# A two-layer hybrid diffusion trunk on one core: transposes held back behind products, and a new order of the last MLP groups and of the tiles that begin the next layer

## The chip, the core and the metric

The kernel runs on one core of a Trainium2 chip. The metric is device microseconds (us) of one execution, as the median of several. Five engines work side by side, each through its own instructions in order: PE (TensorE: matrix products and transposes), DVE (VectorE), ACT (ScalarE), POOL (GpSimd) and SP (SyncE, which issues transfers). An instruction whose operands are not ready holds up everything behind it on its engine.

## The reference, cut to what matters

The program is a trunk of two layers over 1024 latent tokens and a prefix of 256 context tokens, model width 1024, all in fp32.

```
for l in range(DEPTH):                       # DEPTH = 2
    h_lat = rms_norm(x, g_attn_pre[l]) * (1.0 + sc1) + sh1      # h_ctx alike, from ctx
    y_lat, y_ctx = hybrid_mixer(h_lat, h_ctx, not last, w_in[l], ...)
    x = x + gt1 * rms_norm(y_lat, g_attn_post[l])
    h = rms_norm(x, g_mlp_pre[l]) * (1.0 + sc2) + sh2
    x = x + gt2 * rms_norm(sq_relu_mlp(h, w_mlp1[l], w_mlp2[l]), g_mlp_post[l])
    if not last: ctx = ...                   # the same two steps for the context
```

`hybrid_mixer` projects its input once (`w_in`). Four gated DeltaNet heads take q, k, v (after a short convolution and silu; q and k normalized per token) and a gate z; each head solves small triangular systems per chunk of 64 tokens and scans over the chunks. Two more branches take their own columns of the projection: a gated linear recurrence (LRU, gated by a gelu) and a latent attention (MLA, from kv and cq columns). `w_out` joins the branches. The MLP is `square(relu(h @ w1)) @ w2` with 4096 hidden units. Context reads only context, and the last layer makes no context output. The result is the latent stream.

## The kernel before, in words

**Blocks and products.** Tokens lie along the columns, in three blocks: `"c"` (256 context tokens), 0 and 1 (512 latent tokens each); `BL` is c, 0, 1. Every weight tile of 128x1024 is fetched by SP (512 KB), copied by ACT into a high part and subtracted by POOL into a low part (`weight`, L138 on POOL). A product (`mm3`, L230) is 24 matmuls where the contraction is 1024: eight slices, each as high x high, high x low and low x high. In the second MLP projection it is 12 matmuls. A product writes one PSUM bank. The tiles of the input projection rotate over three banks, `mm` (two buffers) and `d` (`pd`).

**Who orders the instructions.** The Python code gives the program order, and a list scheduler with a cost estimate then places each engine's instructions by priority, in program order unless `later(n)` sets a stretch of code back by n. A running engine just follows that list. `put_behind(n, insts)` (L196) ties PE instructions of a side computation to the n-th `mm3` that the program issues after them: they stand right behind that product's last matmul.

**A mixer's input tiles.** `qk_tile` (k with transposed copy, q without) and `v_tile` run a product per block, then per block the convolution on ACT and DVE, `silu2` (DVE `T`, L147), and two or four 128x128 transposes on PE into the one bank `st` (L443 for k and q, L462 for v), which ACT reads. `z_tile`, `gelu_tile` and `kv_tile` have one or two evacuations per block: gelu reads its bank twice on ACT. Per head h, `tiles(h)` issues k, q, v and z, and `head(h)` the head. The heads run one after the other. Each begins with small transposes (L624), has a stretch in which DVE is full (an inversion: DVE `X` L690, then PE `pb` L696), and ends with L821. PE fills in with the tiles of the next head while a head waits.

**The order inside layer 1's mixer.** Before the first head come the two gelu tiles, each for blocks 0 and 1, then z of head 0 for both, then tile 0 (coefficients of all heads and the rope part, `evac` in `mixer`) for blocks 0, 1, c, then k, q and v of head 0. Layer 0 begins with tile 0.

**The norms.** `around(b, ...)` closes a sub-layer for a block: `post` (sums of squares by one-column matmuls, L186; a reciprocal root in eleven small DVE operations; its broadcast back by transposes, L192; then eight times an add and a square) and `prenorm` (the same again, then the next input `A`). `behind` gives the four counts for `put_behind`. After w_out the passes are block 0, then blocks 1 and c together.

**The MLP.** Eight groups g of hidden units, each `up` (four weights) and `down` (four weights). Groups 0 and 1 go by pass, 2 to 5 take all blocks together, and the last two, 6 and 7, go block by block so that each block's norm can run under the next block's products: in layer 0 block 0, then 1, then c, the norm of c falling under the first products of layer 1; in layer 1 block 0, then 1. With c alone, every second weight is split by DVE and not by POOL (`weng`).

Of the kernel before, what the change touches and what calls it, by code (L numbers as in the profile page):

```python
# [43 lines left out]
class Trunk:  # L44
# [386 lines left out]
    def qk_tile(self, L, hs, i, ct, blocks, name, tok=False):  # L431

        d = self.dram(name)
        dt = self.dram(name + "t") if tok else None
        ss = self.sp.tile([P, NCH], F32, name=self.nm("ss"))

        def done(b, acc):
            c0, w = GRP[b]
            th = self.silu2(acc)
            self.keep(d, b, acc)  # L440
            ps = self.G()
            for j in range(w):
                self.nc.tensor.transpose(ps[:, j * P:(j + 1) * P], acc[:, j * P:(j + 1) * P], self.ident)  # L443
            for j in range(w):
                self.act(th[:, j * P:(j + 1) * P], ps[:, j * P:(j + 1) * P], AF.Square, accum_out=ss[:, c0 + j:c0 + j + 1])
            self.ts(ss[:, c0:c0 + w], ss[:, c0:c0 + w], 4 * EPS, ALU.add)
            if tok:
                self.act(th, ps[:, :w * P])
                self.keep(dt, b, th)
        self.conv_tile(L, hs, i, SM["gconv"][0] + 4 * ct, blocks, done)  # L450
        return d, ss, dt

    def v_tile(self, L, hs, i, ct, blocks, name):
# [3 lines left out]
        def done(b, acc):  # L457
            w = GRP[b][1]
            self.silu2(acc)
            ps = self.G()  # L460
            for j in range(w):
                self.nc.tensor.transpose(ps[:, j * P:(j + 1) * P], acc[:, j * P:(j + 1) * P], self.ident)  # L462
            t = self.T()[:, :w * P]
# [34 lines left out]

    def kv_tile(self, L, hs, i, name):

        d = self.dram(name)

        def evac(b, ps):
# [5 lines left out]
            self.keep(d, b, t)  # L509
        self.w_in_tile(L, hs, i, BL, evac)  # L510
        return d

# [522 lines left out]
    def mixer(self, L, hs, obl):  # L1035
# [22 lines left out]
        lg = [self.dram(f"lg{t}") for t in range(2)]  # L1058

        if l:  # L1060
            for t in range(2):
                self.gelu_tile(L, hs, 6 + t, obl, lg[t])
            self.z_tile(L, hs, 8, obl, zd[0])
        self.w_in_tile(L, hs, 0, [0, 1, "c"] if l else BL, evac)
        self.gdn_coeffs(L, ba)
# [5 lines left out]
        def tiles(h):  # L1071
# [3 lines left out]
                       self.v_tile(L, hs, i0 + 2, 3 * h + 2, BL, f"v{h}")))  # L1075
            if h or not l:
                self.z_tile(L, hs, 8 + h, obl, zd[h])

# [5 lines left out]
        def xtile(t):  # L1084
            xg.append((self.lx_tile(L, hs, 4 + t, t, f"lx{t}"), lg[t]))
            if not l:
                self.gelu_tile(L, hs, 6 + t, obl, lg[t])

        def kvq():
            pk["kvn"] = self.kv_tile(L, hs, 1, "kvn")  # L1090
            pk["cqn"] = self.cq_tiles(L, hs, 2, obl, "cqn")
# [6 lines left out]
        head(3)  # L1098
        kvq()
        self.close(self.ap)  # L1100
        side = self.side
# [44 lines left out]
    def layer(self, L, hs, xsrc, xdst_mid, xdst_end, nextL):  # L1146
# [10 lines left out]

        def weng(bl, i):

            return nc.vector if bl == ["c"] and i % 2 else None  # L1160

        def around(b, acc, ss, which, x, dst, Ln, nwhich, behind):


            with self.actor("s", (self.tp, 4), ["a", "b" if which and b == "c" else "d"]):
                s2 = self.post(b, acc, ss, L, which, x, dst, Ln is not None, behind[:2])
# [6 lines left out]
        for bl in passes:  # L1173
# [9 lines left out]
            for b in bl:  # L1183
                h2[b] = around(b, acc[b], ss[b], 0, xs[b], xdst_mid, L, 1,
                               {0: (1, 2, 6, 7) if last else (1, 3, 8, 10), 1: (1, 2, 6, 7), "c": (2, 3, 8, 9)}[b])

# [4 lines left out]
        def up(bl, g):  # L1191
            hid = [{} for _ in range(4)]
            for f in range(4):
                w = self.weight(self.I["w_mlp1"][l, 4 * g + f], weng(bl, f))
                for b in bl:
                    n = BLK[b][1]
                    ps = self.M4(n)
                    self.mm3(ps, w, h2[b], range(KD))

                    big = n == 512 or bl == ["c"]  # L1200
                    a = lp.tile([P, 2, 512] if big else [P, 2, n], F32R, tag="hid" if big else "hidc",
                                bufs=8 if big else 4, name=self.nm("hid"))[:, :, :n]
                    r = self.T(0)[:, :n]
# [7 lines left out]
        def down(bl, g, hid):  # L1211
            for mp_ in range(4):
                w = self.weight(self.I["w_mlp2"][l, g, mp_], weng(bl, mp_))
                for mi in range(2):
# [20 lines left out]
        for g in range(2, NG - 2):  # L1235
            down(obl, g, up(obl, g))
        for bl in [[b] for b in obl[-2:] + obl[:-2]]:
            b = bl[0]
            hid = [up(bl, g) for g in (NG - 2, NG - 1)]
            if b == 0:  # L1240
                xs = {}
            for b2 in ([0, 1] if b == 0 else [b] if b == "c" else []):
                xs[b2] = self.fetch(xdst_mid, b2, self.ap, "Ac" if b2 == "c" else "A", 8 if b2 == "c" else 16)
            ss[b] = self.S(BLK[b][1])
            for g in (NG - 2, NG - 1):
                down(bl, g, hid[g - NG])
            hn[b] = around(b, acc[b], ss[b], 1, xs[b], xdst_end, nextL, 0,
                           {0: (2, 3, 7, 8), 1: (0, 0, 0, 0) if last else (2, 4, 9, 11), "c": (1, 2, 3, 4)}[b])
        self.close(lp)
# [184 lines left out]
```

## Time and profile before

| | |
|---|---|
| median of 3 runs | 3834.73 us (3834.34 to 3836.51) |
| the profiled execution's own time | 3835.08 us |
| its span in the profile | 3833.3 us, so 1.8 us lie around it |
| mean granted clock of TensorE | 0.958 |
| busy: PE, DVE, ACT, POOL | 91%, 55%, 43%, 34% of the span |

The stages of the profiled execution, by the start of their first PE instruction: layer 0's first head 154 us, the last head's end 687 us, w_out from 1003 us, layer 1's first product 2097.4 us, its first head 2205 us, the last head's end 2736 us, w_out from about 2982 us.

How to read the rows: "PE pst L443 <- DVE T L147: 22.1, 12, 2.6" in the table of waits says that PE instructions of line 443 that write `pst` stood idle for 22.1 us in all, 12 times, at most 2.6 us, until DVE had written `T` in line 147. A row of the timeline gives the start, the duration, the instruction with output and inputs, the number run together, and in brackets the idle time ahead of it with what ended it. `pst`, `pa`, `pb`, `pd`, `plr`, `mm` are PSUM banks. In a table by windows, "PEclk" is the clock that TensorE was granted as a share of the full one.

### The profile page before, as it was taken

How to read it: one execution, taken by the hardware profiler on the slowest of the kernel's cores; microseconds unless marked ns; L12 is line 12 of the kernel's file. 1: busy time of each engine (PE TensorE's matmuls, PEld its weight loads, DVE VectorE, ACT ScalarE, POOL GpSimd, SP SyncE). 2: the span in 40 equal slices, each digit the busy share in tenths (PEclk: the TensorE clock that was granted, in tenths of full speed). 3: DMA queues.
4: the chain of work that ended last, by engine and by line, in shares of the span. 5: the costliest groups of instructions: out<-in, count | busy, mean ns of one | idle time of the engine just before them, and what ended most of it. 6: DMA issues, size and time to landing. Idle time of an engine off the chain costs nothing. (4 is left out here: it accounts for less than half of the span.)

```text
span 3833.3 us, 51463 instructions
## 1 busy us (share of the span) xinstructions
PE 3505.4 (91%) x19236; PEld 2741.0 (72%) x19236; DVE 2106.1 (55%) x4351; ACT 1648.3 (43%) x3477; POOL 1314.7 (34%) x919
## 2 busy tenths in 40 slices
PE   5999898798998999999997989996798999999998
PEld 3777687344687888888877777774455778888886
DVE  6667757666265155555266587677576371421124
ACT  3555464455454322212354455544555453222242
POOL 4211311335475211111466321113334674222253
PEclk9999999898999999999998999997798999999998
DMA  5221222232432222232334222212002433311143
GB/s 182 94 83 66 83 97 76 91 100 64 151 105 88 67 83 94 88 94 89 128 109 138 99 81 82 77 65 87 31 24 74 153 107 94 96 47 46 52 139 99
DMA packets 164922, 347.13 MB, mean 91 GB/s; under 512 B 15552, under 2 KB 74304, under 8 KB 164672
## 3 DMA queue, kind: packets, MB, share of 16 engines
q1 hardware_dynamic: 164672, 343.85, 27.6%
q8 instruction: 151, 2.47, 0.3%
q14 instruction: 99, 0.81, 0.1%
HBM read 277.99 MB, written 65.80 MB: 90 GB/s over the span
## 5 line engine op out<-in xcount | busy, mean ns | idle before, releaser
L138 POOL TENSOR_TENSOR wl<-wr,wh 128x1024 fp32r<-128x1024 f32 x280 | 679.9, 2429 | 1664.2 <-ACT wh L135 931.0
L230 PE MATMUL mm<-A,wh 128*128 128x512 f32 (+1 forms) x3008 | 709.9, 379 | 12.3 <-DVE A L138 6.3
L135 ACT ACTIVATE wh<-wr 128x1024 fp32r<-128x1024 f32 x288 | 304.8, 1058 | 833.0 <-PE mm L230 328.1
L230 PEld LDWEIGHTS mm<-A,wh 128*128 128x128 f32 x3008 | 522.9, 194 | 108.0 <-ACT A L135 8.1
L138 DVE TENSOR_TENSOR hid<-T,hid 128x512 fp32r<-128x512 f32 (+1 forms) x160 | 173.1, 1084 | 448.4 <-ACT hid L135 448.4
L230 PE MATMUL mm<-A,wl 128*128 128x512 f32 (+1 forms) x1504 | 360.8, 373 | 1.5 <-DVE wl L138 1.4
L230 PE MATMUL mm<-hid,wh 128*128 128x512 f32 (+1 forms) x1280 | 302.9, 378 | 8.8 <-ACT T L135 6.8
L230 PEld LDWEIGHTS mm<-A,wl 128*128 128x128 f32 x1504 | 259.8, 191 | 48.0 <-DVE wl L138 1.6
L230 PEld LDWEIGHTS mm<-hid,wh 128*128 128x128 f32 x1280 | 227.8, 191 | 57.1 <-ACT T L135 7.3
L147 DVE SCALAR_TENSOR_TENSOR T<-raw,sm,T 128x512 f32<-128x512 f32 (+4 forms) x240 | 182.1, 760 | 45.4 <-ACT raw L135 24.2
L138 DVE TENSOR_TENSOR acc<-acc,mm 128x512 f32<-128x512 f32 (+1 forms) x140 | 88.5, 632 | 214.9 <-PE mm L230 214.2
L230 PE MATMUL pd<-A,wh 128*128 128x512 f32 (+1 forms) x704 | 193.9, 403 | 0.0
L230 PE MATMUL plr<-A,wh 128*128 128x512 f32 (+1 forms) x800 | 185.2, 382 | 0.0
L135 ACT ACTIVATE T<-T 128x512 f32<-128x512 f32 (+1 forms) x243 | 141.6, 583 | 95.2 <-DVE T L147 69.2
L1029 PE MATMUL pd<-Pt,V 128*128 128x512 f32 (+1 forms) x336 | 170.0, 628 | 10.6 <-ACT Pt L135 9.0
L138 POOL TENSOR_TENSOR S<-S,T 128x512 f32<-128x512 f32 (+1 forms) x126 | 163.4, 1299 | 36.7 <-ACT T L135 33.0
L230 PE MATMUL mm<-hid,wl 128*128 128x512 f32 (+1 forms) x640 | 167.2, 379 | 8.1 <-DVE wl L138 8.1
L230 PE MATMUL pb<-A,wh 128*128 128x512 f32 (+1 forms) x800 | 173.0, 367 | 1.2 <-ACT wh L135 1.2
L147 DVE SCALAR_TENSOR_TENSOR ada<-wa,sil,ada 128x256 f32<-128x256 f32 x392 | 168.4, 493 | 7.1 <-DMA wa<-in_w_ada_dram 7.1
L230 PEld LDWEIGHTS plr<-A,wh 128*128 128x128 f32 x800 | 143.6, 188 | 31.2
L230 PE MATMUL plr<-hid,wh 128*128 128x512 f32 (+1 forms) x640 | 153.4, 381 | 13.0 <-DVE hid L138 9.9
L147 DVE SCALAR_TENSOR_TENSOR lr<-lr,lr 128x256 f32<-128x256 f32 x218 | 107.0, 501 | 96.7 <-POOL lr L138 87.6
(365 smaller groups left out, 6843.5 us busy)
## 6 DMA issues: line engine op xcount, KB each, us to landing
wr<-in_w_mlp_dram SPq DMA_DIRECT2D x208, 512.0 KB, 3.5
wa<-in_w_ada_dram SPq DMA_DIRECT2D x96, 512.0 KB, 3.7
wr<-in_w_in_dram SPq DMA_DIRECT2D x48, 512.0 KB, 3.6
wr<-in_w_out_dram SPq DMA_DIRECT2D x32, 512.0 KB, 3.7
A<-y SPq DMA_DIRECT2D x32, 256.0 KB, 3.2
xm<-acc SPq DMA_DIRECT2D x32, 256.0 KB, 3.5
x<-xm SPq DMA_DIRECT2D x16, 512.0 KB, 6.2
kT<-k SPq DMA_DIRECT2D x8, 640.0 KB, 4.2
```

The source lines that it names most:

```text
L135: return self.nc.scalar.activation(out, in_, f, **kw)
L138: return (eng or self.nc.vector).tensor_tensor(out, a, b, op=op)
L147: return self.nc.vector.scalar_tensor_tensor(out, a, s, b, op0=op0, op1=op1)
L230: mm = nc.tensor.matmul(ps, w[wi][:, wk, :], a[:, ai, :], start=n == 0, stop=n == last)
L1029: nc.tensor.matmul(po, V[:, c, :], p, start=ci == 0, stop=ci == len(chunks) - 1)
```

## The change

It has four parts.

- **Transposes.** In `qk_tile` and `v_tile` the transposes go through `put_behind(1 + blocks.index(b), ...)`: those of c stand behind the first product that follows the tile's own, those of block 0 behind the second, of block 1 behind the third (q in layer 1, which has no c, counts 0 and 1). What is still held back at the mixer's end of projections is dropped from the list (`self.held = []`).
- **Last MLP groups of layer 0.** Groups 6 and 7 take c and block 0 together on shared weights (up 6, down 6, up 7, down 7), then block 1 alone (up 6, up 7, down 6, down 7). That is sixteen weight tiles fewer; `weng` goes. The norms are issued for block 0, then c, then, after block 1's products, for block 1. Layer 1 keeps block 0, then 1.
- **First tiles of layer 1.** Block 0 alone of gelu 0, gelu 1 and z of all four heads, then kv of c and 0, then tile 0 for c, 0, 1. The block 1 parts of z, gelu and kv come at the places where these tiles stood before or, for z of head 0, after v of head 0. That is seven weight tiles more.
- **Norms after w_out.** `around` of block 1 stands in `later(60)` and that of c in `later(300)`, with new counts; a pair of PSUM banks changes.

```diff
@@ qk_tile (v_tile alike)
             ps = self.G()
-            for j in range(w):
-                self.nc.tensor.transpose(ps[:, j * P:(j + 1) * P], acc[:, j * P:(j + 1) * P], self.ident)
+            self.put_behind(1 + blocks.index(b), [self.nc.tensor.transpose(
+                ps[:, j * P:(j + 1) * P], acc[:, j * P:(j + 1) * P], self.ident) for j in range(w)])
@@ mixer
+        two = [1] if l else obl
+        pk["kvn"] = self.dram("kvn")
         if l:
             for t in range(2):
-                self.gelu_tile(L, hs, 6 + t, obl, lg[t])
-            self.z_tile(L, hs, 8, obl, zd[0])
-        self.w_in_tile(L, hs, 0, [0, 1, "c"] if l else BL, evac)
+                self.gelu_tile(L, hs, 6 + t, [0], lg[t])
+            for h in range(NH):
+                self.z_tile(L, hs, 8 + h, [0], zd[h])
+            self.kv_tile(L, hs, 1, ["c", 0], pk["kvn"])
+        self.w_in_tile(L, hs, 0, BL, evac)
...
-            if h or not l:
-                self.z_tile(L, hs, 8 + h, obl, zd[h])
+            self.z_tile(L, hs, 8 + h, two, zd[h])
...
-            if not l:
-                self.gelu_tile(L, hs, 6 + t, obl, lg[t])
+            self.gelu_tile(L, hs, 6 + t, two, lg[t])
...
-            pk["kvn"] = self.kv_tile(L, hs, 1, "kvn")
+            self.kv_tile(L, hs, 1, [1] if l else BL, pk["kvn"])
...
         kvq()
+        self.held = []
@@ layer
-            with self.actor("s", (self.tp, 4), ["a", "b" if which and b == "c" else "d"]):
+            with self.actor("s", (self.tp, 4), ["a", "b" if which and b == 1 else "d"]):
...
-                h2[b] = around(b, acc[b], ss[b], 0, xs[b], xdst_mid, L, 1,
-                               {0: (1, 2, 6, 7) if last else (1, 3, 8, 10), 1: (1, 2, 6, 7), "c": (2, 3, 8, 9)}[b])
+                with self.later({0: 0, 1: 60, "c": 300}[b]):
+                    h2[b] = around(b, acc[b], ss[b], 0, xs[b], xdst_mid, L, 1,
+                                   {0: (1, 2, 6, 7) if last else (1, 3, 8, 10), 1: (1, 2, 6, 8), "c": (3, 5, 14, 16)}[b])
...
-        for bl in [[b] for b in obl[-2:] + obl[:-2]]:
-            b = bl[0]
-            hid = [up(bl, g) for g in (NG - 2, NG - 1)]
...
+        for bl in ([[0], [1]] if last else [["c", 0], [1]]):
+            gs = (NG - 2, NG - 1)
+            hid = {g: up(bl, g) for g in gs} if len(bl) == 1 else {}
...
+            for g in gs:
+                down(bl, g, hid.get(g) or up(bl, g))
...
-            hn[b] = around(b, acc[b], ss[b], 1, xs[b], xdst_end, nextL, 0,
-                           {0: (2, 3, 7, 8), 1: (0, 0, 0, 0) if last else (2, 4, 9, 11), "c": (1, 2, 3, 4)}[b])
+            for b in bl[::-1]:
+                hn[b] = around(b, acc[b], ss[b], 1, xs[b], xdst_end, nextL, 0,
+                               {0: (2, 3, 7, 8) if last else (1, 2, 6, 7), 1: (0, 0, 0, 0) if last else (1, 2, 6, 7),
+                                "c": (2, 3, 9, 11)}[b])
```

The order of the instructions shows three places. The first is PE in layer 0's mixer, at the k tile of head 0, before. `pst_781` are the two transposes of its context block; `pd_746` is the tile's own last product (block 1), `mm_840` the first product of the next tile, q.

```order
L230 MATMUL pd_746<-A_490,wl_691 128x512
L230 MATMUL pd_746<-A_494,wl_691 128x512
L443 MATMUL pst_781<-cst,T_772 128x128 x2
L230 MATMUL mm_840<-A_402,wh_836 128x256
L230 MATMUL mm_840<-A_406,wh_836 128x256
```

The same transposes now, as `pst_782`; `mm_841` is the q tile's first product and `mm_867` its second.

```order
L230 MATMUL mm_841<-A_426,wl_838 128x256
L230 MATMUL mm_841<-A_430,wl_838 128x256
L443 MATMUL pst_782<-cst,T_773 128x128 x2
L230 MATMUL mm_867<-A_434,wh_837 128x512
L230 MATMUL mm_867<-A_438,wh_837 128x512
```

They have moved past one product of 24 matmuls. Those of blocks 0 and 1 stand behind the second and the third product of q in the same way.

The second place is ACT at the first products of layer 1, before. `T<-mm_17854` and `T<-pd_17888` are the first readings of the two products of gelu 0, blocks 0 and 1; the rows `T<-acc` are the squares of the norm of c (256 columns).

```order
L135 ACTIVATE T_17879<-mm_17854 128x512
L135 ACTIVATE wh_17998<-wr_17996 128x1024
L135 ACTIVATE T_17913<-pd_17888 128x512
L135 ACTIVATE S_17718<-acc_10313 128x256
L135 ACTIVATE T_17726<-acc_10314 128x256
L135 ACTIVATE T_17732<-acc_10315 128x256
L135 ACTIVATE T_17738<-acc_10316 128x256
L135 ACTIVATE T_17744<-acc_10317 128x256
L135 ACTIVATE T_17750<-acc_10318 128x256
L135 ACTIVATE T_17756<-acc_10319 128x256
L135 ACTIVATE T_17762<-acc_10320 128x256
L135 ACTIVATE T_17880<-mm_17854 128x512
```

In the order of after, the same engine at the same place: `mm_17759` is gelu 0 and `pd_17799` gelu 1, both of block 0, and the squares belong to block 1 (512 columns).

```order
L135 ACTIVATE T_17824<-pd_17799 128x512
L135 ACTIVATE S_17618<-acc_10329 128x512
L135 ACTIVATE T_17626<-acc_10330 128x512
L135 ACTIVATE wh_17909<-wr_17907 128x1024
L135 ACTIVATE T_17632<-acc_10331 128x512
L135 ACTIVATE T_17638<-acc_10332 128x512
L135 ACTIVATE T_17644<-acc_10333 128x512
L135 ACTIVATE T_17650<-acc_10334 128x512
L135 ACTIVATE T_17656<-acc_10335 128x512
L135 ACTIVATE T_17662<-acc_10336 128x512
L135 ACTIVATE T_17785<-mm_17759 128x512
L135 ACTIVATE T_17825<-pd_17799 128x512
```

In both orders the second reading of the first gelu product (before `T_17880<-mm_17854`, after `T_17785<-mm_17759`) stands behind all squares of the norm that runs there. The norm is another one, with rows twice as long.

The third place is DVE a little later in layer 1, before. `acc<-acc,pa` are the adds of the norm of c, `A<-acc` its last results; the rows `T<-T,T` belong to gelu and z.

```order
L138 TENSOR_TENSOR acc_10319<-acc_10319,pa_17784 128x256
L138 TENSOR_TENSOR acc_10320<-acc_10320,pa_17784 128x256
L144 TENSOR_SCALAR acc_10319<-acc_10319,mod_118,ada_117 128x256
L147 SCALAR_TENSOR_TENSOR T_17954<-T_17954,T_17953 128x512
L138 TENSOR_TENSOR A_17803<-acc_10316,A_17803 128x256
L147 SCALAR_TENSOR_TENSOR T_17988<-T_17988,T_17987 128x512
L138 TENSOR_TENSOR A_17823<-acc_10320,A_17823 128x256
```

Now, with the norm of block 1 (`pa_17686`) and, behind it, the reciprocal root for kv of c (`n4s<-pst_18016`):

```order
L138 TENSOR_TENSOR acc_10335<-acc_10335,pa_17686 128x512
L138 TENSOR_TENSOR acc_10336<-acc_10336,pa_17686 128x512
L144 TENSOR_SCALAR acc_10335<-acc_10335,mod_118,ada_117 128x512
L138 TENSOR_TENSOR A_17707<-acc_10332,A_17707 128x512
L144 TENSOR_SCALAR n4s_18019<-pst_18016 128x2
L156 TENSOR_SCALAR n4s_18020<-n4s_18019 128x2
L143 TENSOR_SCALAR n4s_18022<-n4s_18019 128x2
L138 TENSOR_TENSOR n4s_18021<-n4s_18020,n4s_18022 128x2
```

The root of kv, for which PE's broadcast `pst_18035` waits, stands behind the adds of block 1's second norm step.

## Prediction of the time, made before the changed kernel was run

> **What bounds the kernel now.** The page first: PE is busy for 91% of the span. Its work is the same in both kernels, so what can be won or lost is PE's idle time, 3833.3 - 3505.4 = 328 us, and the time it runs at a lower clock.
>
> ```profile
> span 3833.3 us, 51463 instructions
> PE 3505.4 (91%) x19236; PEld 2741.0 (72%) x19236; DVE 2106.1 (55%) x4351; ACT 1648.3 (43%) x3477; POOL 1314.7 (34%) x919
> ```
>
> Then the table of what PE waited for, in the groups that the change can reach (total, times, longest).
>
> ```profile
> PE pb L696 <- DVE X L690: 34.3, 8, 10.5
> PE pst L443 <- DVE T L147: 22.1, 12, 2.6
> PE plr L230 <- DVE hid L138: 9.9, 1, 9.9
> PE mm L230 <- DVE wl L138: 9.5, 2, 8.1
> PE pst L462 <- DVE T L147: 11.6, 7, 2.1
> PE mm L230 <- ACT T L135: 6.8, 1, 6.8
> ```
>
> The transposes (`pst` L443, L462) are 22.1 + 11.6 = 33.7 us; the single waits `plr`, `mm <- DVE wl` and `mm <- ACT T` lie at the ends of sub-layers. Then a table by stretches (length; busy PE, PEld, DVE, ACT, POOL; granted clock; DMA): the norms after w_out in layer 0, the end of layer 0, the first products of layer 1, layer 1's four heads, layer 1's attention.
>
> ```profile
> 1123.90:1203.10 79.20, 68.33 (x294) 53.85 (x294) 70.50 (x116) 48.82 (x80) 56.92 (x37) 0.96 0.34 110
> 1968.00:2098.00 130.00, 105.52 (x620) 94.09 (x619) 88.07 (x122) 65.78 (x102) 82.27 (x47) 0.89 0.39 126
> 2097.40:2136.00 38.60, 33.02 (x135) 26.10 (x134) 21.70 (x54) 14.35 (x26) 24.23 (x22) 0.91 0.31 98
> 2205.00:2736.00 531.00, 442.71 (x3614) 359.42 (x3613) 384.97 (x981) 272.45 (x768) 117.93 (x99) 0.90 0.22 74
> 2740.00:2982.00 242.00, 216.06 (x715) 127.21 (x714) 160.39 (x276) 124.27 (x253) 97.59 (x115) 0.91 0.15 46
> ```
>
> In the first three PE loses its idle time plus (1 - clock) times its busy time: 79.2 - 68.33 + 0.04 x 68.33 = 13.6; 24.5 + 0.11 x 105.52 = 36.1; 5.6 + 0.09 x 33.02 = 8.6. Together **58.3 us**. In the heads PE is 83% busy at clock 0.90: no engine is full there on the mean, and the four heads follow one another as a chain. Layer 1's time is then set by when its first head starts.
>
> **What a wait costs in clock.** PE's timeline behind two long waits, and at full rate just ahead of layer 1's first head:
>
> ```profile
> 2057.98 0.58 PE L230 MATMUL plr<-hid,wh 128*128 128x256 f32 x1 [9.95 <-DVE hid L138]
> ...
> 2060.78 2.05 PE L230 MATMUL pb<-hid,wh 128*128 128x256 f32 x8
> ...
> 2110.30 0.38 PE L192 MATMUL pa<-cst,n4s 128*128 128x128 f32 x2
> ...
> 2120.91 1.01 PE L186 MATMUL pb<-ones,S 128*128 128x1 f32 x4 [4.61 <-POOL S L138]
> 2121.78 6.54 PE L230 MATMUL mm<-A,wh 128*128 128x512 f32 x16
> ...
> 2198.84 3.91 PE L230 MATMUL pd<-A,wh 128*128 128x512 f32 x16
> 2202.59 2.04 PE L230 MATMUL pd<-A,wl 128*128 128x512 f32 x8
> ...
> 2204.69 0.38 PE L624 MATMUL pa<-cst,gv 128*128 128x128 f32 x2
> ```
>
> Eight 256-column matmuls take 2.05 us behind the wait of 9.95; sixteen of 512 columns, four times the work, take 3.91 at full rate, so 2.05 is half rate. The 16 matmuls behind the wait of 4.61 take 6.54, 2.6 more than 3.91. I put 3 us beside each wait of 5 to 12 us.
>
> The Trainium skill, in "TensorE: Matmul & The Clock Gate" (What's actually happening), states that an idle window of about 3.4 us halves the clock until one such window of work has passed, so 1.7 us a time, an estimate from that page; the row of 6.54 shows more, and counts. The rule speaks against the next part: two waits of 2 us leave the clock alone, one of 4 us does not, and if five heads lose 1.7 us so, the sum would be 3829 - 3 + 8.5, about 3835, by it.
>
> **Transposes.** The timeline of PE shows the waits that the counts are to remove, and one after them (`pb` L696).
>
> ```profile
> 125.02 0.65 PE L443 MATMUL pst<-cst,T 128*128 128x128 f32 x4 [1.25 <-DVE T L147]
> ...
> 141.73 0.66 PE L462 MATMUL pst<-cst,T 128*128 128x128 f32 x4 [1.69 <-DVE T L147]
> ...
> 204.31 0.66 PE L443 MATMUL pst<-cst,T 128*128 128x128 f32 x4 [2.18 <-DVE T L147]
> ...
> 221.59 0.22 PE L696 MATMUL pb<-X,N 32*32 32x32 f32 x2 [1.57 <-DVE X L690]
> ...
> 531.79 0.65 PE L443 MATMUL pst<-cst,T 128*128 128x128 f32 x4 [2.33 <-DVE T L147]
> ...
> 549.68 0.66 PE L462 MATMUL pst<-cst,T 128*128 128x128 f32 x4 [1.70 <-DVE T L147]
> ...
> 2179.09 0.66 PE L443 MATMUL pst<-cst,T 128*128 128x128 f32 x4 [1.07 <-DVE T L147]
> ...
> 2192.16 0.66 PE L443 MATMUL pst<-cst,T 128*128 128x128 f32 x4 [1.69 <-DVE T L147]
> ```
>
> The transposes now stand 24 to 72 matmuls later, by which time DVE has long written `T`. But most of the 33.7 us lie inside a head's inversion. There DVE is full from L681 to L690, and PE needs its `X` at L696. At 204.31 PE waits 2.18 for `T`, and at 221.59 still 1.57 for `X`: what is saved at the first is waited for at the second, since PE fills in with the same products ahead of L696. The order bears that out: up to L696 of the first three heads PE has 114.2, 182.0 and 247.1 us of projection work where it had 114.3, 183.2 and 249.2. I count only waits outside an inversion: ahead of layer 0's head 0, 1.25 + 1.69 = **-2.9**; ahead of layer 1's head 0, 1.07 + 1.69 = **-2.8**; between heads 2 and 3 of layer 0, 2.33 + 1.70 = 4.0, from which 3.1 us go for fill-in work that now stands ahead of head 3 (26.1 us by the order, 23.0 before): **-0.9**. The `T` buffers are held up to 72 matmuls longer; DVE and ACT, which would wait for them, have that long a lead, so I cost it at nothing, at 6 us if the lead is gone. The merged waits at L696 cost clock. How much no row shows directly; bounds from the rows on the clock are 0 and, with 1 us for each of eight heads, 8, since much of what follows L696 is small work at which PE waits anyway; I take **+3**.
>
> **The ends of the sub-layers.** *Norms after w_out.* Those of c and block 1 yield to the MLP's own evacuations. Of the 13.6 us, 6.8 is one wait for ACT's `T`, which stood behind them. I leave 3 (1 to 8). What covers the later norms is block 0's MLP work.
>
> *End of layer 0.* The long waits for `hid` and `wl` (9.95 and 8.06) belong to c alone, which goes: c now shares weights with block 0. Sixteen weight loads go too; PE doesn't wait for weights elsewhere there. But the norms of 0 and then c now fall under block 1's up products, in almost the positions, counted in matmuls, that c's and 1's had after w_out before, and here nothing yields. I take the same loss, 13.6 (3 to 20).
>
> *First products of layer 1.* Block 1's norm now runs here in place of c's. The order of ACT puts the second reading of gelu 0's bank behind the norm's eight squares. There are three banks, so the fourth product, z of head 1, waits for that reading. The broadcast in PE's timeline, then in ACT's the last square of a 512-column norm, of c's, and the reading behind it:
>
> ```profile
> 1941.07 0.60 PE L192 MATMUL pa<-cst,n4s 128*128 128x128 f32 x4
> ```
>
> ```profile
> 1957.80 0.64 ACT L135 ACTIVATE T<-acc 128x512 f32<-128x512 f32 x1 [1.06 <-POOL S L138]
> ...
> 2119.57 0.42 ACT L135 ACTIVATE T<-acc 128x256 f32<-128x256 f32 x1 [0.45 <-DVE acc L147]
> 2120.09 0.60 ACT L135 ACTIVATE T<-mm 128x512 f32<-128x512 f32 x1
> ```
>
> A 512-column norm took 1958.44 - 1941.07 = 17.4 us from broadcast to last square, c's 2119.99 - 2110.30 = 9.7. The third product fills 5.6 us of it. So c's gave 9.7 + 0.6 - 5.7 = 4.6, as measured at 2120.91, and block 1's gives 17.4 + 0.6 - 5.7 = 12.3, with 3 of clock 15 (0 to 22). Behind it kv of c needs a reciprocal root on DVE, which the order puts behind the adds of block 1's second norm step.
>
> ```profile
> 2039.48 4.22 DVE L147 SCALAR_TENSOR_TENSOR acc<-acc,mod,x 128x512 f32<-128x512 f32 x2
> ...
> 2121.96 0.16 DVE L144 TENSOR_SCALAR n4s<-pb 128x2 f32<-128x2 f32 x1 [2.49 <-PE pb L186]
> ...
> 2122.43 2.44 DVE L138 TENSOR_TENSOR n4s<-n4s,n4s 128x2 f32<-128x2 f32 x2
> ...
> 2126.08 0.16 DVE L147 SCALAR_TENSOR_TENSOR n4s<-n4s,n4s 128x2 f32<-128x2 f32 x1
> ...
> 2132.81 0.74 DVE L138 TENSOR_TENSOR acc<-acc,pa 128x256 f32<-128x256 f32 x2
> 2133.47 0.83 DVE L144 TENSOR_SCALAR acc<-acc,mod,ada 128x256 f32<-128x256 f32 x1
> ```
>
> That step takes c 0.74 + 0.83 = 1.57 for two adds and a scaling, so for 512 columns and four such sets about 4 x 2 x 1.57 = 12.6 us; the root's chain took 2126.24 - 2121.96 = 4.3. PE comes to the broadcast for it after 10 us (24 matmuls of 512 columns, 24 of 256, 7 of 512). So 12.6 + 4.3 - 10 = 7 us, 8 with a second wait behind it, with 3 of clock 11 (2 to 15). Smaller waits: 2. Together 3 + 13.6 + 15 + 11 + 2 = 44.6 against 58.3: **-13.7**.
>
> **Layer 1's order.** PE's work before the first head (L624 at 2204.69 above) is counted in products of 24 matmuls. One of 512 columns takes 2204.63 - 2198.84, less the overlap of its last matmul, 5.6, one of 256 columns 2.8. Before: gelu 4, z 2, tile 0, k and v 2.5 each, q 2, in all 15.5 products of 512 columns, 86.8 us. Now gelu 2, z 4, kv 1.5, the same 9.5, and block 1 of z of head 0, in all 18, 100.8. The first head starts 14.0 us later; it can't start sooner, since its operands come last on PE. This is a cost: afterwards the chain of heads sets the pace, and the work brought forward would have filled PE's idle time there. **+14.0.** Seven more weight tiles cost POOL this much each:
>
> ```profile
> L138 POOL TENSOR_TENSOR wl<-wr,wh 128x1024 fp32r<-128x1024 f32 x280 | 679.9, 2429 | 1664.2 <-ACT wh L135 931.0
> ```
>
> That is 17 us on an engine that is 22% busy in the heads; covered. In return kv and cq leave the last head's cycle, and the LRU can begin earlier; attention (242 us, PE 216 busy) may shorten, while head 3's inversion gets about 6 us more of DVE work by the order. I take **-2** (-8 to +4).
>
> Nothing of this lies on SP: its queue issues nine weight tiles fewer, and none of PE's waits above is one for a transfer.
>
> **Sum.** -2.9 - 2.8 - 0.9 + 3 - 13.7 + 14 - 2 = -5.3. The execution's own time is 3835.1 (span plus 1.8), so 3829.8; the median lies 0.4 below it: **3829**.
>
> **The rivals.**
> *All transposes' waits are won.* If DVE gets to `X` sooner too, because PE's earlier products feed it earlier, another 33.7 - 9.7 = 24 us go, and the 3 of clock: 3802. For it: the waits are the largest group after L696. Against: DVE is full there.
> *The boundary stalls don't come.* If z of head 1 finds its bank free and kv's root isn't late, 15 + 11 go: 3803. For it: the 17.4 us held a weight copy and other readings on ACT between the squares; at layer 1's start fewer compete. Against: ACT's order.
> *Slower: block 1's norm is drawn out by POOL.* Under it POOL subtracts seven weight tiles. At 2122.43 two tiny DVE operations took 2.44, as long as one POOL subtraction (2.43), and at 2039.48 two of 512 columns 4.22, where four times the 0.83 of 256 columns is 3.3. If each of the four pairs in both steps of that norm pays one, this is 8 x 2.4 = 19 us ahead of layer 1's first head: 3848. It decides once the broadcast lies over 22 us before gelu 0's second reading. The Trainium skill, "SBUF — State Buffer" (Who interferes with whom), says that a DVE operation with two SBUF inputs and a reading GpSimd one exclude each other; these rows agree.
> *The change does not do what it says.* The scheduler places norms and transposes so that the same waits return elsewhere and layer 1's order has no price: 3834.
>
> **How the numbers follow.** Within 0.2%, 7.7 us, is about what a measurement of this kernel can't tell from no change: 3827.0 to 3842.4. Chances: forecast 0.38, transposes 0.12, no stalls 0.20, slower 0.22, nothing 0.08. The forecast's own range, from bounds that partly cancel, is 3820 to 3840; of its 0.38, 0.14 lie below 3827, 0.21 within, 0.03 above. Faster 0.14 + 0.12 + 0.20 = 0.46; same 0.21 + 0.08 = 0.29; slower 0.03 + 0.22 = 0.25. The range takes in the cases at 3802 and 3848: 3800 to 3850.
>
> **What would show it.** Right: `pst` L443 and L462 nearly gone from PE's waits while L696's total grows by some 20 us; layer 1's first L624 about 14 us further behind its first product, plus the stalls; a wait of about 12 us at z of head 1 in layer 1; waits of 5 to 7 us under block 1's last groups. Wrong: no growth at L696; no wait over 3 us in layer 1's first 50 us; heads that end earlier in layer 1 than their start was delayed.

## The result, and the profile after

The changed kernel takes 3885.27 us (median of 4 runs, 3881.41 to 3889.30) where the kernel before, run beside it, takes 3835.62. The ratio is 1.0125, with a 95% interval of 1.0107 to 1.0143: **slower by 1.25%**, 48 us. The forecast was 3829 and the range ended at 3850.

The profiled execution took 3881.41 us. The page of the changed kernel, its first rows:

```profile
span 3879.5 us, 51346 instructions
PE 3511.4 (91%) x19236; PEld 2749.1 (71%) x19236; DVE 2103.9 (54%) x4343; ACT 1634.0 (42%) x3468; POOL 1303.8 (34%) x918
```

PE did the same matmuls in nearly the same busy time, so it waits 368 us now, 40 more. What it waited for (total, times, longest):

```profile
PE pb L696 <- DVE X L690: 45.6, 8, 9.3
PE plr L847 <- ACT lr L135: 24.4, 2, 23.1
PE mm L230 <- ACT T L135: 23.0, 7, 12.3
PE plr L847 <- DMA lr<-lx: 13.8, 4, 11.2
PE pd L186 <- POOL S L138: 13.7, 5, 4.6
PE pst L443 <- DVE T L147: 7.7, 6, 2.6
PE pst L463 <- DVE T L147: 5.4, 4, 3.4
```

The transposes' own waits fell from 33.7 us to 7.7 + 5.4 = 13.1, and L696 rose from 34.3 to 45.6. At `plr` L847, the products of the LRU, the wait of 24.4 us for ACT is new, the one for the transfer of `lx` was 3.4 us before and is 13.8 now, and `mm <- ACT T` grew from 6.8 to 23.0. By stretches (length; busy PE, PEld, DVE, ACT, POOL; granted clock), the norms after w_out in layer 0, the end of layer 0, layer 1 up to its first head, layer 1's heads:

```profile
1145.10:1240.00 94.90, 84.38 (x359) 67.21 (x358) 61.60 (x111) 48.87 (x77) 59.01 (x34) 0.95 0.34 109
1990.00:2100.60 110.60, 101.17 (x446) 80.64 (x445) 82.21 (x134) 58.95 (x91) 81.28 (x52) 0.97 0.32 107
2100.60:2237.10 136.50, 115.55 (x559) 94.00 (x559) 77.25 (x162) 57.13 (x122) 54.87 (x33) 0.92 0.32 105
2237.10:2786.70 549.60, 431.03 (x3539) 350.48 (x3538) 401.72 (x978) 282.07 (x794) 142.89 (x126) 0.87 0.22 74
```

Set beside the same stages of before, the profiled executions differ so (each figure from the first row of a stage in PE's timeline; the first products of layer 1 are at 2097.4 and 2100.6):

| stage | before | after | difference |
|---|---|---|---|
| start to the end of layer 0's heads | 687.1 | 704.5 | +17.4 |
| from there to layer 1's first product | 1410.3 | 1396.1 | -14.2 |
| from there to layer 1's first head | 107.3 | 136.5 | +29.2 |
| layer 1's four heads | 531.3 | 549.6 | +18.3 |
| the rest of the span | 1097.3 | 1092.8 | -4.5 |

Part of the first difference is chance. Up to w_out the order of the instructions is that of before in ten of the kept kernels, before included, and their layer 0 heads ended at 687.1 to 694.5 us, 690.7 in the mean; it is that of after in four (after, e1, e13, e16 below), and theirs ended at 692.4 to 704.5, 699.2 in the mean. So some 8 us of the 17.4 go with the order; before was the earliest of its ten and after the latest of its four.

The rows that the prediction named for layer 1's start, in PE's timeline of after:

```profile
2059.30 2.93 PE L230 MATMUL mm<-hid,wh 128*128 128x512 f32 x6 [6.84 <-ACT T L135]
...
2131.35 5.62 PE L230 MATMUL mm<-A,wh 128*128 128x512 f32 x16 [12.33 <-ACT T L135]
...
2171.13 0.66 PE L192 MATMUL pst<-cst,n4s 128*128 128x128 f32 x2 [4.87 <-DVE n4s L147]
...
2237.14 0.38 PE L624 MATMUL pa<-cst,gv 128*128 128x128 f32 x2
```

The first is the end of layer 0 (6.84, the same wait as after w_out before), the second z of head 1 (12.33), the third the broadcast for kv (4.87), the last the first head. They stand where they were expected, at nearly their forecast size. The loss that was not expected lies for the most part elsewhere: in layer 0's heads, in layer 1's heads, and in norms that were to gain.

### The profile page after: what moved, and what is told of

The parts are those of the page before. It is cut to its first block, busy times and chain, and to the rows that moved or that the text cites. A ratio compares the mean times of both kernels' runs of the same rounds, so it can differ in the third digit from the quotient of the medians.

```text
span 3879.5 us, 51346 instructions
## 1 busy us (share of the span) xinstructions
PE 3511.4 (91%) x19236; PEld 2749.1 (71%) x19236; DVE 2103.9 (54%) x4343; ACT 1634.0 (42%) x3468; POOL 1303.8 (34%) x918
## 3 DMA queue, kind: packets, MB, share of 16 engines
q1 hardware_dynamic: 163376, 339.13, 26.9%
## 5 line engine op out<-in xcount | busy, mean ns | idle before, releaser
L135 ACT ACTIVATE wh<-wr 128x1024 fp32r<-128x1024 f32 x279 | 295.2, 1058 | 835.1 <-PE mm L230 347.4
L138 DVE TENSOR_TENSOR hid<-T,hid 128x512 fp32r<-128x512 f32 (+1 forms) x160 | 163.2, 1021 | 487.8 <-ACT hid L135 487.6
L230 PEld LDWEIGHTS pb<-A,wh 128*128 128x128 f32 x800 | 138.6, 190 | 27.9 <-ACT wh L135 0.6
```

The lines of the kernel that those rows point to most:

```text
L135: return self.nc.scalar.activation(out, in_, f, **kw)
L138: return (eng or self.nc.vector).tensor_tensor(out, a, b, op=op)
L230: mm = nc.tensor.matmul(ps, w[wi][:, wk, :], a[:, ai, :], start=n == 0, stop=n == last)
```

## The experiments

Every kernel was run against the kernel before on the same chip. Single executions of one kernel scatter by some 10 us on either side, so what a few us mean is read from the ratio of many runs, and where they lie from the profiles.

**The parts one by one.** e1 is before with the held-back transposes alone, e2 the change without them, e3 before with the norms after w_out alone, e4 before with the two new orders (last groups, layer 1's first tiles) alone. The change of a pair of PSUM banks concerns the norms after the MLP, so it is in e4 and not in e3.

> The kernel before with the held-back transposes alone. Theory A (the loss is a sum of separate pieces, the transposes lengthen the heads): heads of layer 0 end about 19 us later, those of layer 1 take about 6 us more, so about 3860 us. Theory B (the prediction's: most waits only move to L696, the rest is won): 3831 us, heads as long as before or shorter. Theory C (transposes hurt only together with the new order of layer 1): layer 0 loses its 19 us all the same by the trace, layer 1 nothing: 3854 us.

> The changed kernel with the transposes put back where they were. Theory A: the 25 us of the first experiment go, about 3860 us, layer 0's last head ends at 687 us as before; head 3 of layer 1 stays about 13 us longer than before, since its PE queue holds early LRU products. Theory B: 3889 us, a few us slower than the change. Theory C: 3850 us, since head 3's loss goes as well.

> The kernel before with the yielding norms after w_out and their new counts alone. Theory A (from the two traces): nothing won in layer 0, where the waits of 10.8 us only change their places, and about 11 us lost in layer 1, so 3846 us. Theory B (the prediction's): 10 us won in layer 0, nothing lost in layer 1, 3825 us.

> The kernel before with the new order of the last groups and of layer 1's first tiles alone (no held-back transposes, norms after w_out as before). Theory A: 22 us won at the end of layer 0, 32 us later at layer 1's first head, 13 us lost in head 3, 17 us won in the attention: 3841 us. Theory B (the prediction's terms for these parts, -13.7 + 14 - 2): 3833 us. Theory C: the chain's loss in head 3 doesn't come, 3828 us.

| | median, us | ratio to before (95%) |
|---|---|---|
| e1 transposes | 3845.99 | 1.0020 (1.0006 to 1.0034) |
| e2 change without transposes | 3872.69 | 1.0092 (1.0072 to 1.0112) |
| e3 norms after w_out | 3849.39 | 1.0029 (1.0019 to 1.0040) |
| e4 orders | 3858.83 | 1.0055 (1.0036 to 1.0073) |

The parts give 0.20 + 0.29 + 0.55 = 1.04% against 1.25% for the whole, so within their intervals the loss is a sum of separate pieces; e2's 0.92% fits 0.29 + 0.55 too. The prediction's terms were -3.6 us for e1, -10.6 for e3 and +9 for e4 (3.1 won at the boundaries, 14 lost, 2 won). Measured: about +8, +11 and +21. All three were too low. My 25 us for e1, read from one profile, was too high; e1's own profiled execution was one of its quickest, 3836.16 us, so its profile by itself shows almost no loss.

**Where the transposes lose.** e8 holds back only q and k (in `v_tile` the old loop stands); e9 holds back all, but puts v's copy into the buffer that is free; e13 and e14 hold back all in one layer.

```diff
 # e9, in v_tile
-            self.silu2(acc)
+            th = self.silu2(acc)
...
-            t = self.T()[:, :w * P]
+            t = th
 # e13 (e14: L.l == 1)
-            self.put_behind(1 + blocks.index(b), [...])
+            self.put_behind(1 + blocks.index(b) if L.l == 0 else 0, [...])
```

> The kernel before with the transposes of q and k held back and those of v where they were. Theory A (v's late transposes, which fall into the next head's opening, make the loss): openings of layer 0's heads 0 and 3 back to 21 us from 25 and 27, 3837 us. Theory B (q and k cost as well, by the T buffers that they hold longer): openings still over 24 us, 3843 us. The prediction's theory: 3832 us.

> All transposes held back as in the first experiment, but v's transposed copy goes into the buffer that silu2 left free, so that a block of v takes one T buffer less. Theory A (v's late transposes cost because z's evacuations stand on ACT waiting for T buffers that v's copies still hold, and the next head's opening stands behind them): openings of layer 0's heads 0 and 3 go from 25.6 and 27.2 back under 23 us, about 3836 us. Theory B (the opening is long because the transposes themselves stand at its beginning): openings as in the first experiment, 3845 us.

> The kernel before with all transposes held back in layer 0 alone. Theory A (the loss is that of layer 0's openings, heads 0 and 3, about 4 and 6 us, as in the profiles): 3845 us, as the first experiment. Theory B (the loss lies in layer 1): 3835 us.

> The kernel before with all transposes held back in layer 1 alone. Theory A (loss in layer 0): 3832 us, a few us under the kernel before, since PE waits less ahead of head 0 and head 3's inversion has no LRU rows. Theory B (loss in layer 1): 3845 us.

| | median, us | ratio to before (95%) |
|---|---|---|
| e8 q and k only | 3835.61 | 0.9991 (0.9979 to 1.0003) |
| e9 v's copy in place | 3845.89 | 1.0025 (1.0015 to 1.0035) |
| e13 layer 0 only | 3842.17 | 1.0027 (1.0014 to 1.0040) |
| e14 layer 1 only | 3829.62 | 0.9981 (0.9972 to 0.9990) |

Held back in layer 0 alone, the transposes cost about 0.27%, 10 us (0.12% if the medians are compared); in layer 1 alone they win 0.19%, 7 us. With q and k alone there is no difference that these runs can tell, and e1 and e8, which differ in v alone, lie 0.29% apart. So the loss needs v's transposes, and it is in layer 0. In layer 0 the place is a head's opening, from its first small transpose on PE (L624, here L625 or L626) to the first row of its inversion on DVE (`X<-C`). e13, PE then DVE:

```profile
149.78 0.38 PE L626 MATMUL pa<-cst,gv 128*128 128x128 f32 x2
```

```profile
174.94 2.10 DVE L683 STREAM_TRANSPOSE X<-C 128x1024 f32<-128x1024 f32 x1 [1.07 <-ACT C L135]
```

and e14, whose layer 0 is that of before:

```profile
156.33 0.38 PE L626 MATMUL pa<-cst,gv 128*128 128x128 f32 x2
```

```profile
177.40 2.07 DVE L683 STREAM_TRANSPOSE X<-C 128x1024 f32<-128x1024 f32 x1 [1.05 <-POOL qT L138]
```

and e8, with q and k alone:

```profile
153.17 0.38 PE L625 MATMUL pa<-cst,gv 128*128 128x128 f32 x2
```

```profile
174.99 2.07 DVE L682 STREAM_TRANSPOSE X<-C 128x1024 f32<-128x1024 f32 x1 [1.05 <-POOL qT L138]
```

With all held back head 0 starts earlier (149.78) and its opening takes 25.2 us, with none 21.1, with q and k alone 21.8; head 3's takes 26.9, 21.4 and 22.1 in the same three executions. This doesn't hang on the scatter: the openings of heads 0 and 3 are 25.2 to 25.8 and 26.8 to 27.4 us in the four kernels with that order, 21.1 to 21.4 both in the ten with the old one. Most of what the earlier start won is given back, and head 3 loses 5.5 more. The rows of ACT in head 0's opening, before:

```profile
154.90 0.68 ACT L135 ACTIVATE T<-pd,der 128x512 f32<-128x512 f32 x1
...
158.25 1.28 ACT L135 ACTIVATE at<-at,gv 128x128 f32<-128x128 f32 x4 [0.97 <-DVE at L138]
...
159.92 1.26 ACT L135 ACTIVATE at<-at,gv 128x128 f32<-128x128 f32 x4
```

and after:

```profile
156.11 1.27 ACT L135 ACTIVATE at<-at,gv 128x128 f32<-128x128 f32 x4
157.28 0.58 ACT L135 ACTIVATE T<-pa 128x512 f32<-128x512 f32 x1
159.53 0.69 ACT L135 ACTIVATE T<-mm,der 128x512 f32<-128x512 f32 x1 [1.67 <-DMA v<-T]
160.12 0.68 ACT L135 ACTIVATE T<-pd,der 128x512 f32<-128x512 f32 x1
160.69 1.27 ACT L135 ACTIVATE at<-at,gv 128x128 f32<-128x128 f32 x4
```

`at<-at` is the head's own work; the two sets of four are block 0's, and the second of them is the one that moved. Before, the last reading of z, `T<-pd,der` at 154.90, comes ahead of all this, and the second set comes 5.72 us after the head's start (159.92 - 154.20). After, two readings of z stand right in front of it, the first waits 1.67 us until the transfer of v's copy has freed a T buffer, and the set comes 8.47 us after the start (160.69 - 152.22). That is 2.75 of the 4 us. ACT's waits for v's transfers from 104 to 750 us went from 1.5 to 5.7 us. But e9, which takes one T buffer less for a block of v, brought the openings to 23.9 and 26.0 us only and the time nowhere. So the crowded buffer is a part of it; that the late work of the v and z tiles now stands in the head's opening is shown, which of its pieces decides is not.

**The norms after w_out.** e5 is e3 with layer 1 as before; e10 is e3 with larger counts.

```diff
 # e5
-                with self.later({0: 0, 1: 60, "c": 300}[b]):
+                with self.later({0: 0, 1: 0 if last else 60, "c": 300}[b]):
 # ... and 1: (1, 2, 6, 7 if last else 8)
 # e10
-                                   ... 1: (1, 2, 6, 8), "c": (3, 5, 14, 16)}[b])
+                                   ... 1: (1, 2, 9, 11), "c": (3, 5, 18, 20)}[b])
```

> The kernel before with the yielding norms after w_out in layer 0 alone; layer 1 keeps its priorities and counts. Theory A (the loss of the third experiment lies in layer 1, where the sums of block 1 stand a fixed number of products behind a broadcast that now comes later): 3838 us, as the kernel before, and no wait of 4.6 us for POOL's S in layer 1. Theory B (layer 0 costs as much): 3844 us. The prediction's own term: 3826 us.

> The norms after w_out as in the third experiment, with the second step's sums and broadcast of block 1 and of c three to four products further behind. Theory A (the yielding norm is fine, but its counts leave POOL too little time, so PE waits for S): the waits of 4.6 us in both layers go and with them the lost clock; 3849 falls to about 3834 us, slightly under the kernel before. Theory B (the yielding moves other work, whatever the counts): 3848 us.

e5 took 3843.12 us, ratio 1.0011 (1.0002 to 1.0020), and e10 3836.18, ratio 1.0003 (0.9991 to 1.0015). e3 stood at 1.0029. So about two thirds of e3's loss lie in layer 1, as far as these intervals tell, and the larger counts take all of it away, but win nothing. The mechanism is in PE's rows for block 1 in layer 1: the broadcast (L192) and the next sums (L186) of before,

```profile
3097.42 0.62 PE L192 MATMUL pa<-cst,n4s 128*128 128x128 f32 x4 [0.40 <-DVE n4s L147]
...
3120.27 0.95 PE L186 MATMUL pd<-ones,S 128*128 128x1 f32 x8
```

of e3 (the broadcast comes in four rows; the first stands here),

```profile
3105.70 0.27 PE L192 MATMUL pa<-cst,n4s 128*128 128x128 f32 x1
...
3128.68 1.87 PE L186 MATMUL pd<-ones,S 128*128 128x1 f32 x8 [4.65 <-POOL S L138]
```

and of e10:

```profile
3099.76 0.27 PE L192 MATMUL pa<-cst,n4s 128*128 128x128 f32 x1
...
3131.92 0.95 PE L186 MATMUL pd<-ones,S 128*128 128x1 f32 x8
```

The second step's sums stand a fixed number of products behind the broadcast. Before, the broadcast is 22.9 us ahead of them and PE doesn't wait at them. In e3 it yields and comes late, so the same count leaves only 3124.0 - 3105.7 = 18.3 us of products, and PE waits 4.65 for POOL's `S`: the norm takes 3128.68 - 3105.70 = 23.0. In e10 there are 32.2 us and no wait. That settles why it lost; e10's missing gain is the other half: the 6.8 us for ACT's `T` are gone in layer 0 as forecast, but by its trace PE waits there 6.0 for a broadcast, where it was 1.8, and 3.7 for `S` instead.

**Layer 1's first head.** e7 is e4 with both gelu buffers from the half that the squares don't use; e11 is e7 with z of heads 1 to 3 back at their old places; e16 is the whole change with only those z tiles put back.

```diff
 # e7, in gelu_tile
-            g, q = self.T()[:, :ps.shape[-1]], self.T()[:, :ps.shape[-1]]
+            g, q = self.T(0)[:, :ps.shape[-1]], self.T(0)[:, :ps.shape[-1]]
 # e11 and e16, in mixer
-            for h in range(NH):
-                self.z_tile(L, hs, 8 + h, [0], zd[h])
+            self.z_tile(L, hs, 8, [0], zd[0])
...
-            self.z_tile(L, hs, 8 + h, two, zd[h])
+            self.z_tile(L, hs, 8 + h, obl if h else two, zd[h])
```

> The order-only kernel with both buffers of a gelu tile taken from the half of the T buffers that the norm's squares do not use. Theory A (gelu's second reading stands behind the squares only because its buffer comes after theirs in the rotation, and this wait is the 12 us at z of head 1): that wait goes, layer 1's first head starts 15 us earlier, 3844 us. Theory B (the wait moves on, to z of head 3 or to kv's root): under 5 us won, 3855 us.

> The kernel of the seventh experiment with only z of head 0 brought ahead; z of heads 1 to 3 at their old places for all blocks: three products less ahead of layer 1's first head. Theory A (work ahead of the first head is paid in full, 5.6 us a product): first head 17 us earlier, less what block 1's norm, then with less cover, makes PE wait at tile 0, about 12 us: 3848 us. Theory B (the first head waits for block 1's norm anyway): first head no earlier, 3852 us. If the LRU, which no longer comes early then, costs: 3860 us.

> The whole change with one part undone: z of heads 1 to 3 at their old places for all blocks. Theory A (work ahead of the first head is paid in full, and with it back in the heads the LRU no longer enters head 3's inversion): the 27 us between the seventh and the eleventh experiment go here too, 3858 us, with an inversion of head 3 under 35 us. Theory B (only the 17 us of the products' own size go, because here the gelu tiles still wait behind the norm's squares): 3868 us. Theory C (norm of block 1 then waits uncovered): 3880 us.

e7 took 3852.42 us, ratio 1.0037 (1.0025 to 1.0049), 0.18% under e4, though the two intervals overlap. Its PE at layer 1's start:

```profile
2112.37 4.02 PE L230 MATMUL mm<-A,wh 128*128 128x512 f32 x16 [3.24 <-ACT T L135]
...
2210.88 0.38 PE L622 MATMUL pa<-cst,gv 128*128 128x128 f32 x2
```

The wait, 12.33 us in e4 as in the change, is down to 3.24: gelu's second reading stood behind the squares only because its buffer came after theirs in the rotation. Part of the gain moved on: at the two broadcasts behind it PE waits 4.18 and 3.56 us, in e4 1.30 and 4.86. From layer 1's first product to its first head e7 takes 131.3 us, e4 142.2.

e11 took 3825.39, ratio **0.9970** (0.9958 to 0.9982): faster than before, and 0.67%, 26 us, under e7. That is more than any of its theories gave (3848 at best).

```profile
2196.34 0.38 PE L622 MATMUL pa<-cst,gv 128*128 128x128 f32 x2
```

Its first head starts 14.5 us ahead of e7's, for three products of 5.6 us: work ahead of the first head is paid nearly in full. The four heads take 519.7 us and not 546.3, and the rest 15 more. And e16 against the change itself, 3845.77 us, ratio 1.0024 (1.0013 to 1.0035) against 1.0125: three z products put back win **1.0%, 39 us**, the largest single piece and 12 us more than expected. In its profile layer 1's first head comes 18.2 us earlier after layer 0's heads, the four heads take 512.7 us and not 549.6, and the rest takes 25.0 more. (Another 6.8 us lie in layer 0's heads, where the order is the same, so they are scatter.)

**Head 3 and the LRU.** The 36.9 us (549.6 - 512.7) in e16's heads come on top of the products, which now lie within them. About half is head 3: 135.6 us and not 153.8, with an inversion of 31.8 and not 55.1. The other half lies in heads 0 to 2, and no run here shows why. For head 3, the table of busy time for the rows of the LRU alone (`lr`; PE, PEld, DVE, ACT, POOL), within the inversion of layer 1's last head, is this before:

```profile
2614.00:2660.00 46.00, 3.88 (x8) 2.30 (x8) 1.13 (x3) 5.54 (x13) 4.03 (x5) 0.70 0.26 85
```

in e4, and what PE waited for there:

```profile
2641.80:2699.20 57.40, 7.40 (x16) 4.58 (x16) 13.78 (x28) 14.40 (x32) 21.07 (x28) 0.53 0.10 30
```

```profile
PE plr L845 <- ACT lr L135: 22.7, 2, 19.5
PE plr L845 <- DMA lr<-lx: 11.3, 1, 11.3
```

and in e11:

```profile
2603.80:2636.20 32.40, 2.05 (x4) 1.22 (x4) 0.00 (x0) 2.13 (x5) 0.00 (x0) 0.78 0.23 76
```

In e4 28 DVE rows and 28 of POOL enter the inversion, PE stands 34 us behind LRU products, and the inversion takes 57.3 us; in before it takes 44.7, in e11 with none of these DVE rows 32.4. In e4 PE has no projection left between head 3's L624 and L696, by the order of its instructions (62 matmuls before, 86 in e11), so the scheduler put the LRU there. e6 holds the LRU products of e4 behind that inversion:

```diff
 # e6, in lru's segment; self.mark is the last matmul of the inversion
+                if L.l:
+                    self.tc.add_manual_dep(mi.ins, self.mark.ins.name, ...)
```

> The order-only kernel of the fourth experiment with layer 1's LRU products (L847 of the kernel before) held behind PE's products of head 3's inversion, so that DVE has no LRU rows in that inversion (25 before). Theory A (LRU work in DVE's queue lengthens the inversion and with it the chain): inversion from 57 to about 35 us, head 3 from 148 to about 128, attention longer by some 10, so about 3848 us. Theory B (that work has to be done anyway and the stretch after the heads is bound by it): head 3 shorter, the attention longer by the same, 3859 us.

It took 3876.39 us, ratio 1.0091 (1.0074 to 1.0107): 0.36%, 14 us, **slower** than e4. The inversion fell to 40.5 us and head 3 from 148.3 to 132.8, but by its profile the time behind the heads rose by 30, from 1087.6 to 1117.9. Both theories fell, mine by sign: holding the early LRU back costs more behind the heads than it wins in them, and which piece loses it there isn't shown. From layer 1's first head to the end the profiles have 1634 us in e4, 1650 in e6, 1629 before, 1624 in e11, 1631 in e16, 1642 in the change: a good part of what the heads win is given back behind them, and the earlier first head is won besides.

**The change mended, and a better kernel.** e12 is the change with e9's, e10's and e7's edits together. e15 is e11 with the transposes of q and k held back as in e8.

> The whole change with three mendings: v's copy in place, the larger counts after w_out, and gelu's buffers from the free half. If the three causes add up as the single experiments say, 3885 - 10 - 12 - 6 = 3857 us; if they hide one another, 3870 us or more. No theory here expects it under the kernel before, since the work ahead of layer 1's first head and the longer chain of heads stay.

> The kernel of the eleventh experiment with the transposes of q and k held back as in the eighth. If both gains add up: 3825 - 2 = 3823 us. If the held transposes only trade waits: 3825 us. If they push more fill-in work into layer 1's last head, with the LRU later still: 3832 us.

e12 took 3855.61 us, ratio 1.0056 (1.0038 to 1.0074), where the sum of the causes said 3857. That agreement is partly luck: 10 us of the 28 in that sum were for v's copy, and e9, run beside e12, won nothing. By their ratios e7, e9 and e10 won 0.18, -0.05 and 0.26%, together 0.39% or 15 us, and e12 is 0.69% under the change. e15 took **3821.65 us, ratio 0.9961 (0.9946 to 0.9975)**, 15 us under the kernel before and 64 under the change; its interval overlaps e11's, so the held transposes' share in that isn't shown. It keeps the new order of layer 0's last groups with block 1's norm under layer 1's first tiles, brings only gelu, z of head 0 and kv ahead, and leaves the norms after w_out alone.

## Why the prediction was wrong

By its own steps, in their order.

**Transposes: -3.6 us forecast, +8 measured.** That most of the waits only move to L696 held in layer 0: there they fell from 17.9 us to 5.1 and L696 rose from 14.8 to 22.5, in the change as in e13. In layer 1 it failed to the good side: in e1, with nothing else changed, they fell from 15.7 to 8.0 and L696 fell too, from 19.5 to 12.8. That head 0 of layer 0 starts earlier held (149 to 152 us against 154). The step that failed is "DVE and ACT ... have that long a lead, so I cost it at nothing": in layer 0 the late work of v and z stands in the next head's opening, which I had not costed at all, and the openings of heads 0 and 3 take 4 and 5.5 us longer. That the price of 6 us was named for the case that the lead is gone, and left out of the sum, was the mistake. In layer 1 the forecast's sign was right (e14, -7).

**Norms after w_out: -10.6 forecast, +11 measured.** The failed step is "I leave 3 (1 to 8)". It removed a wait and didn't ask what was late next: the sums, which stand by a count of products and not by time. The forecast put a gain on a wait that was known and nothing on the count that the change itself had moved the broadcast against.

**End of layer 0 and first products of layer 1: nearly right.** In the two windows the loss at layer 0's end fell from 36.1 to 9.4 + 0.03 x 101.17 = 12.5 us, against 13.6 forecast. The wait at z was 12.33 (12.3), kv's 4.87 (7). From first product to first head it is 29.2 us more; the forecast's terms, 14 + 15 + 11 + 2 - 8.6 - 2.8, make 30.6. In e4's profile, which has these parts alone, 18.6 us are won from layer 0's heads to layer 1's first product where 22.5 were forecast, and 34.9 are lost from there to the first head where the terms without the transposes' make 33.4.

**Layer 1's order: +14 forecast, right for the start, too small for the whole.** e11 and e16 confirm the price of work ahead of the first head. The step "-2 (-8 to +4)" for the heads and what follows failed: in the change they took 18.3 - 4.5 = 13.8 us more, of which by e3 and e5 about 7 belong to w_out's norms in layer 1; in e4's profile 5.0 more. I had taken the earlier LRU as a gain and the work that leaves head 3's cycle as relief; in fact it left PE without projections to fill head 3's inversion, which grew from 44.7 us to 55.1.

Of the rivals, "all transposes' waits are won" and "the boundary stalls don't come" are refuted by the rows above. "Block 1's norm is drawn out by POOL" gave the right direction for a wrong reason: by its own sign the broadcast had to lie over 22 us before gelu 0's second reading, and it lay 17.9 (2112.80 to 2130.70). One row behind it was misread as well: at 2122.43 POOL wasn't subtracting a weight tile, its two operations on `T` of 2.51 us in all ran there. "The change does not do what it says" was right that waits after w_out return elsewhere, wrong that layer 1's order has no price. The range ended at 3850 because all costs outside that one mechanism were bounded by the forecast's own small terms.

On the clock the Trainium skill did better than my rows at the waits that came. In "TensorE: Matmul & The Clock Gate" (What's actually happening) it gives about 3.4 us at half rate behind a long idle window, an estimate of 1.7 us lost. Behind the wait of 12.33 the 16 matmuls from 2131.35 took 5.62 us where 3.91 is full rate, so 1.7; behind those of 6.84 and 4.87 eight took 3.78 and 3.76 where 2.03 is full rate, so 1.7 again. I had put 3.

## What to carry to other kernels

Work brought ahead of a serial chain to cover something short is paid nearly in full at the chain's start, and the chain then lacks it as fill-in: count both ends. Where an instruction is placed by a count of other instructions, moving its producer by priority changes the time that the count buys, so re-derive the count. When a wait is moved, cost the queue that it moves into on every engine, not only the engine that stopped waiting.

## What the runs showed of the hardware

The same instructions in the same order took different times from one execution to the next: the order on all five engines up to layer 0's w_out is the same in the change and in e1, and the last of layer 0's heads ended at 704.5 and 692.4 us in their two profiles. A difference of 10 us in one stage of one pair of profiles is therefore no proof; the ratios over ten runs told e1's 0.20% and e8's -0.09% apart.
